# Three ordering edits in a hybrid decoder trunk: the first matmul of each product kept behind the product ahead, the MLP's first weight sum put in front of the operand sums, and the second MLP matrix's first weights issued from GpSimd's queue

## The chip, the cores and the metric

The kernel runs on one core of one Trainium2 chip. The metric is the device time of one execution in microseconds (us), lower is better. Engines are named as the profile names them: PE is TensorE (matmul), ACT is ScalarE, DVE is VectorE, POOL is GpSimd and SP is SyncE. POOL and SP here mostly issue DMA transfers, each into a queue of its own.

## What is computed

One layer: token mixing (a short causal convolution beside forgetting attention, merged by gates), then a squared-ReLU MLP, each with a residual. SEQ is 512, D_MODEL 2048, D_FF 8192, all in float32. The part that matters here, cut down:

```python
merged = gc * conv_branch + ga * attn_branch
x = x + jnp.einsum('bsd,de->bse', merged, w_mix_out[l])          # "mix" below
h = rmsnorm(x, g_mlp[l])
u = jnp.square(jax.nn.relu(jnp.einsum('bsd,df->bsf', h, w_ff1[l])))   # "ff1"
x = x + jnp.einsum('bsf,fd->bsd', u, w_ff2[l])                    # "ff2"
return rmsnorm(x, g_final)
```

## The kernel before

**Seven products for eight.** Each large matrix product is cut in 2x2 quarters and done with seven block products (the Strassen-Winograd form). On the activation side the seven operands are named A11, A12, A22 and the sums S1 to S4; on the weight side the quarters are tiles `x00`, `x01`, `x10`, `x11` (`y..` in ff2), and their sums are made in place by subtractions on DVE (L113). The PSUM accumulators are named `a`, `b`, `c`, `d`, and the results are combined in SBUF tiles `o`.

**Two parts for float32.** Each operand is split in a high part and a low part. `split` (L101) does that: ACT copies the tile to a rounded high part (L103, `th` for weights), and DVE subtracts it from the tile for the low part (L104, `tl`). A product is then three groups of matmuls: high by high and high by the activation's low part, pair by pair, and at the end the weight's low part by the activation's high part. In `mm_rows` these are L172, L173 and L175 (the activation is the stationary operand), in `mm_cols` L153, L155 and L157 (the weight is). So a product needs `th` at its first matmul and `tl` only two thirds on; `th` and `tl` have two buffers each, which come free when the matmuls that read them are done.

**Stages around the change.** The product with `w_mix_out` runs as four column groups of class `Group` (mix groups 0 to 3), the one with `w_ff1` as 16 groups (ff1 groups 0 to 15; the first is `g0`), the one with `w_ff2` as units `unit(seg, cg)`. A mix group runs `head` (A11 into `a`, A12 into `b`) and `tail3` (S1 into `c`, S2 into `a`, S4 into `c`, S3 into `d`, A22 into `a`). S4's low-part result and S2's accumulator meet in `plus` (L116): `o<-c` on ACT (L233), then `o<-a,o` on DVE, and only then A22 may start bank `a` anew. `g0` runs `head`, then `tail2`: S1 into `c`, S3 into `d`, S2 into `a`, S4, A22.

**How ff1 gets its operands.** The result of each mix group is turned (`turn`, transposes on PE into `ptr`), scaled into tiles `f`, and from them class `Mix` makes the operands of ff1: `first_of` is the sum `s1`, `sums` makes the others, `out` splits them. The first three mix groups' shares go through memory (`h_d`, `f_d`) and are loaded again by `begin_part` on POOL's queue; the last group's share is added on chip. For A11 and A12 the loaded rows are split by `split_part` (`A12<-A12 128x1536` on ACT L103 and DVE L104). ff1's weights of `g0` are loaded on POOL's queue too (`g0.queue`, issued at L208). The first weight sum of `g0`, `x00 = x01 - x00`, is in `first_sum`; the mean of the squares, `mean`, is one small matmul (L1308) with a reduction behind it.

**ff1 to ff2.** `put_u` squares the results, makes the sums of ff2's operands in tiles `r`, splits them (`rh` on ACT, `r<-r,rh 128x1792` on DVE L1218) and stores them to `s_d` on POOL's queue. `load_sums` brings them back as `us` tiles (L1337), on POOL's queue as well: part 0 before the last ff1 group's tail, part 1 behind it, then parts 2 and 3. The weights of `unit` come as four tiles of 1 MB each, `y00`, `y10`, `y01`, `y11` (L1438), all on SP's queue before. The first unit runs A11 into `a`, A12 into `b`, S2 into `a` (its weight is `t2 = y11 - (y01 - y00)`), then `d` with `y01 = y11 - y01`.

**What sets the order.** The program is written in a tile framework. A scheduler chooses the order on each engine by its own estimates, within the dependences; `tc.keep_in_program_order(ins)` ties an instruction to the place it has in the code against the others that are tied so, and `tc.issue_after` sets another lower bound. Each engine then runs its list strictly in order, waiting on semaphores. The steps that hang on a product (`after`, class `Steps`) are called when that product's matmuls have been written.

Of the kernel before, what the change touches and what calls it, by code (L numbers as in the profile page):

```python
# [15 lines left out]
P = 128  # L16
# [29 lines left out]
def tile_hybrid_block(ctx: ExitStack, tc, x, g_mix, w_in, b_f, b_gate, conv_w, w_conv_out,  # L46
# [87 lines left out]
        bank(i, "lay")  # L134


    def mm_cols(ps, Sx, hi, lo, first, extra=None):


        ps = ps[0].rearrange("p (j s) -> p j s", j=2)  # L140
        nq = hi.shape[1]
        for part in range(2):
            for q in range(nq):
                Sh, Sl = Sx(q)
                if extra == "first" and part == 0 and q == 0:
                    nc.tensor.matmul(ps[:, 0, :192], hi[:, q, :P], Sh[:, :192], start=True, stop=False,
                                     skip_group_check=True)
                elif extra and extra != "first" and part == 0:
                    extra(q, Sh, hi[:, q, :])
                for j in range(2):  # L150
                    o, js = ps[:, j, :], slice(j * P, (j + 1) * P)
                    if part == 0:
                        nc.tensor.matmul(o, hi[:, q, js], Sh, start=first and q == 0 and j == 0, stop=False,  # L153
                                         skip_group_check=True)
                        nc.tensor.matmul(o, hi[:, q, js], Sl, start=False, stop=False, skip_group_check=True)  # L155
                    else:
                        nc.tensor.matmul(o, lo[:, q, js], Sh, start=False, stop=q == nq - 1, skip_group_check=True)  # L157

    def mm_rows(ps, Sx, hi, lo, first, extra=None, blocks=range(2), qs=None):

        nq, w = hi.shape[1], hi.shape[2]
        for b in blocks:
            o = ps[b][:, :w] if len(ps) == 2 else ps[0][:, b * w:(b + 1) * w]
            begin = first and (b == 0 or len(ps) == 2)
            ts = slice(b * P, (b + 1) * P)
            for part in range(2):
                for q in qs or range(nq):
                    Sh, Sl = (e[:, ts] for e in Sx(q))
                    if extra == "first" and part == 0 and q == 0 and b == 0:
                        nc.tensor.matmul(o[:, :192], Sh, hi[:, q, :192], start=True, stop=False, skip_group_check=True)  # L170
                    if part == 0:
                        nc.tensor.matmul(o, Sh, hi[:, q, :], start=begin and q == 0, stop=False, skip_group_check=True)  # L172
                        nc.tensor.matmul(o, Sl, hi[:, q, :], start=False, stop=False, skip_group_check=True)  # L173
                    else:
                        nc.tensor.matmul(o, Sh, lo[:, q, :], start=False, stop=q == nq - 1, skip_group_check=True)  # L175
# [14 lines left out]
    class Group:  # L190
# [3 lines left out]
        def __init__(self, view, c1, c2, w, ST, mm, banks, put, scale=1.0, extra={}, after=None, shift=SHIFT):  # L194
            self.extra, self.after, self.shift = extra, {} if after is None else after, shift
            self.view, self.cs, self.w, self.ST, self.mm, self.banks = view, (c1, c2), w, ST, mm, banks
            self.put, self.scale, self.at = put, scale, {}
            self.begun, self.queue, self.X = False, nc.sync, {}
# [15 lines left out]
        def run(self, ps, n, src, first):  # L214
            hi, lo = parts([P, self.nq, self.w], self.shift if self.w == HS else 0)
            split(src, hi, lo)
            if n in self.mid:
                self.mm(ps, self.ST(n), hi, lo, first, blocks=(0,))
                self.mid[n]()
                self.mm(ps, self.ST(n), hi, lo, first, blocks=(1,))  # L220
            elif n in self.extra:
                self.mm(ps, self.ST(n), hi, lo, first, self.extra[n])
            else:
                self.mm(ps, self.ST(n), hi, lo, first)
            self.after.get(n, lambda: None)()

        def room(self, i, j):
# [870 lines left out]
    class Mix:  # L1098
# [158 lines left out]
    for g in range(4):  # L1257
# [42 lines left out]
    def factors(common, r):  # L1300
# [122 lines left out]
    def unit(seg, cg, ST):  # L1423
# [9 lines left out]
        for i, j in ((0, 1), (1, 1), (0, 0), (1, 0)) if end else ((0, 0), (1, 0), (0, 1), (1, 1)):  # L1433
# [137 lines left out]
```

## Time and profile before

| | us |
|---|---|
| median of 3 runs (range) | 2443.41 (2442.65 to 2449.26) |
| the profiled execution: its own time | 2446.44 |
| its span in the trace | 2444.7 |
| PE busy | 2408.0 (98%) |
| DVE busy | 2042.6 (84%) |
| ACT busy | 1203.9 (49%) |
| POOL busy | 277.9 (11%) |

The page of the profile gives busy time by engine and the chain that ended last. A row of the timeline reads: start, duration, engine, line, operation, tile written<-tile read, shape, and in brackets how long the engine had been idle before it and what ended that. A matmul's duration is modelled and longer than the distance to the next one; what counts is the distance from start to start, 0.113 us for 256 columns and 0.227 us for 512 where PE waits for nothing. A row of the DMA view ends with the time from issue to landing. A row of the windows view has the stretch, its length, the busy time of PE, of the weight load, DVE, ACT and POOL (each with its count), then the clock that was granted to PE (1.00 is full), the DMA engines' busy share and GB/s. 1.7 us of the execution lie outside the span.

### The profile page before, as it was taken

To read this page: it belongs to the slowest core of one execution; us is meant where nothing else is said; L and a number is where in the kernel's file an instruction comes from. 1 tells how busy PE (TensorE), PEld (TensorE's weight loads), DVE (VectorE), ACT (ScalarE), POOL (GpSimd) and SP (SyncE) were. 2 spreads that over 40 slices of the span, in tenths; PEclk is the share of its full clock that TensorE was granted. 3 is DMA by queue.
4 is the path that set the end of the run, shared out by engine and by line. 5 is a ranking of instruction groups with operands and counts; after the bars stand their busy time and mean duration, and the time that the engine had idled before them with its cause. 6 is when DMAs were issued, how large, how long until landed. Compare 5 with 4: busy or idle time off the path is not lost.

```text
span 2444.7 us, 41518 instructions
## 1 busy us (share of the span) xinstructions
PE 2408.0 (98%) x17800; PEld 2265.2 (93%) x17800; DVE 2042.6 (84%) x1718; ACT 1203.9 (49%) x1233; POOL 277.9 (11%) x446
## 2 busy tenths in 40 slices
PE   8999999999999999999899999999999999999998
PEld 8999899999999999899899999999997888888886
DVE  7987777788888778888889898898888888889898
ACT  6443434345455435355656665666655333333334
POOL 0100000111121111112300000000011001100000
PEclk9999999999999999999999999999999999999999
DMA  7664544445656665657854655646587566655662
GB/s 251 183 191 143 154 134 144 142 154 168 216 170 215 209 208 171 214 163 254 311 198 162 227 204 199 235 171 227 206 301 273 168 240 233 232 194 178 248 224 103
DMA packets 283916, 489.87 MB, mean 200 GB/s; under 512 B 11772, under 2 KB 195188, under 8 KB 283348
## 3 DMA queue, kind: packets, MB, share of 16 engines
q1 hardware_dynamic: 232912, 279.01, 36.0%
q0 software_dynamic: 49952, 207.12, 22.9%
q8 instruction: 139, 2.28, 0.4%
q10 hardware_dynamic: 868, 1.10, 0.1%
q14 instruction: 45, 0.37, 0.0%
HBM read 377.60 MB, written 109.05 MB: 199 GB/s over the span
## 4 chain that ended last, share of the span: by engine, by line
PE 90%; DVE 4%; issue 2%; DMA 2%; ACT 1%; POOL 1%; SPq 0%; DVEq 0%; POOLq 0%; ACTq 0%
PE a L157 6%; PE a L153 6%; PE a L155 6%; PE a L175 5%; PE a L173 5%; PE a L172 5%; PE d L153 5%; PE d L155 5%; PE d L157 5%; PE c L153 4%; PE c L155 4%; PE c L157 4%; PE d L175 3%; PE d L173 3%; PE d L172 3%; PE b L153 3%
## 5 line engine op out<-in xcount | busy, mean ns | idle before, releaser
L103 ACT ACTIVATE th<-x 128x2048 fp32r<-128x2048 f32 (+1 forms) x280 | 537.0, 1918 | 509.2 <-DVE x L113 168.9
L104 DVE TENSOR_TENSOR tl<-x,th 128x2048 fp32r<-128x2048 f32 (+1 forms) x280 | 639.5, 2289 | 168.8 <-ACT th L103 153.8
L113 DVE TENSOR_TENSOR x<-x,x 128x2048 f32<-128x2048 f32 (+1 forms) x160 | 366.1, 2288 | 21.2 <-DMA x<-in_w_in_dram 17.1
L103 ACT ACTIVATE th<-y 128x2048 fp32r<-128x2048 f32 (+1 forms) x109 | 185.4, 1701 | 273.0 <-PE a L173 138.6
L104 DVE TENSOR_TENSOR tl<-y,th 128x2048 fp32r<-128x2048 f32 (+1 forms) x109 | 219.1, 2014 | 30.0 <-ACT th L103 29.6
L172 PE MATMUL a<-th,us 128*128 128x512 f32 x512 | 199.3, 389 | 2.0 <-ACT th L103 2.0
L173 PE MATMUL a<-th,us 128*128 128x512 f32 x512 | 199.2, 389 | 0.0
L153 PE MATMUL c<-S,th 128*128 128x256 f32 x848 | 196.8, 277 | 0.6 <-ACT th L103 0.6
L155 PE MATMUL c<-S,th 128*128 128x256 f32 x848 | 196.4, 277 | 0.0
L153 PE MATMUL a<-S,th 128*128 128x256 f32 x784 | 182.6, 278 | 0.0
L155 PE MATMUL a<-S,th 128*128 128x256 f32 x784 | 181.2, 277 | 0.0
L153 PEld LDWEIGHTS c<-S,th 128*128 128x128 f32 x848 | 159.4, 188 | 1.0 <-ACT th L103 0.7
L155 PEld LDWEIGHTS c<-S,th 128*128 128x128 f32 x848 | 159.4, 188 | 0.0
L155 PEld LDWEIGHTS a<-S,th 128*128 128x128 f32 x784 | 147.4, 188 | 0.0
L153 PEld LDWEIGHTS a<-S,th 128*128 128x128 f32 x784 | 147.3, 188 | 0.0
L175 PE MATMUL a<-tl,us 128*128 128x512 f32 x512 | 137.0, 390 | 0.6 <-DVE tl L104 0.6
L153 PE MATMUL d<-S,th 128*128 128x256 f32 x544 | 128.0, 280 | 0.0
L155 PE MATMUL d<-S,th 128*128 128x256 f32 x544 | 127.3, 279 | 0.0
L155 PE MATMUL b<-A,th 128*128 128x256 f32 x544 | 126.7, 278 | 0.0
L153 PE MATMUL b<-A,th 128*128 128x256 f32 x544 | 126.7, 278 | 0.0
L153 PE MATMUL a<-A,th 128*128 128x256 f32 x544 | 126.3, 278 | 0.0
L155 PE MATMUL a<-A,th 128*128 128x256 f32 x544 | 126.2, 277 | 0.0
(387 smaller groups left out, 6065.8 us busy)
## 6 DMA issues: line engine op xcount, KB each, us to landing
x<-in_w_in_dram SPq DMA_DIRECT2D x86, 1024.0 KB, 6.0
y<-in_w_ff_dram SPq DMA_DIRECT2D x64, 1024.0 KB, 7.0
x<-in_w_ff_dram SPq DMA_DIRECT2D x60, 1024.0 KB, 8.3
us<-s_d POOLq DMA_DIRECT2D x48, 1024.0 KB, 9.9
s_d<-rh POOLq DMA_DIRECT2D x32, 896.0 KB, 5.2
s_d<-r POOLq DMA_DIRECT2D x32, 896.0 KB, 6.1
x<-in_w_mix_out_dram SPq DMA_DIRECT2D x17, 1024.0 KB, 6.7
g_d<-o POOLq DMA_DIRECT2D x32, 256.0 KB, 2.7
```

The source lines that it names most:

```text
L103: a = nc.scalar.activation(out=hi, in_=src, func=AF.Copy, scale=one)
L104: b = nc.vector.tensor_tensor(out=lo, in0=src, in1=hi.bitcast(F32), op=ALU.subtract)
L113: return nc.vector.tensor_tensor(out=out, in0=a, in1=b, op=ALU.subtract)
L153: nc.tensor.matmul(o, hi[:, q, js], Sh, start=first and q == 0 and j == 0, stop=False, skip_group_check=True)
L155: nc.tensor.matmul(o, hi[:, q, js], Sl, start=False, stop=False, skip_group_check=True)
L157: nc.tensor.matmul(o, lo[:, q, js], Sh, start=False, stop=q == nq - 1, skip_group_check=True)
L172: nc.tensor.matmul(o, Sh, hi[:, q, :], start=begin and q == 0, stop=False, skip_group_check=True)
L173: nc.tensor.matmul(o, Sl, hi[:, q, :], start=False, stop=False, skip_group_check=True)
L175: nc.tensor.matmul(o, Sh, lo[:, q, :], start=False, stop=q == nq - 1, skip_group_check=True)
```

## The change

There are three edits.

1. `pinned` keeps the first matmul of a product in program order while `pin[0]` is set. `Group.run` sets it for groups with `in_order`: the four mix groups and `g0`. So a product's first matmul can no longer be put among the matmuls of the product ahead of it.
2. `first_of` of the last mix group is tied behind `first_sum`, so `x00 = x01 - x00` stands ahead of `s1` and what follows it. In mix group 3, `split_part("A12")` moves from the steps after A22 to the steps after S3, ahead of the load of `x10`.
3. The first unit of ff2 issues its four weight loads on POOL's queue; the others stay on SP's.

```diff
+    pin = [False]
+    def pinned(ins):
+        if pin[0]:
+            tc.keep_in_program_order(ins)
+            pin[0] = False
...
-                        nc.tensor.matmul(o, Sh, hi[:, q, :], start=begin and q == 0, stop=False, skip_group_check=True)
+                        pinned(nc.tensor.matmul(o, Sh, hi[:, q, :], start=begin and q == 0, stop=False,
+                                                skip_group_check=True))
...
             split(src, hi, lo)
+            pin[0] = self.in_order
...
+            pin[0] = False
             self.after.get(n, lambda: None)()
...
         def first_of(self):
             self.s1 = pm.tile([P, 2, HS], F32, tag="s1", name="s1")
-            add(self.s1, self.F[1][:, 0], self.F[1][:, 1])
+            return nc.vector.tensor_tensor(out=self.s1, in0=self.F[1][:, 0], in1=self.F[1][:, 1], op=ALU.add)
...
-    g0.queue = nc.gpsimd
+    g0.queue, g0.in_order = nc.gpsimd, True
...
+            after.add("S3", lambda: split_part("A12"))
             after.add("S4", lambda: split_part("A11"))
             after.add("S3", lambda: g0.ahead(1, 0), lambda: begin_part("S3", 3))
             after.add("A22", lambda: g0.ahead(0, 1))
-            after.add("A22", lambda: split_part("A12"))
         group = groups[g]
+        group.in_order = True
...
-    g0.after = Steps(A11=[lambda: g0.ahead(1, 1), turn_waiting, begin_rest, lambda: first_sum_after(mix.added), mix.first_of],
+    g0.after = Steps(A11=[lambda: g0.ahead(1, 1), turn_waiting, begin_rest, lambda: first_sum_after(mix.added),
+                          lambda: tc.keep_in_program_order(mix.first_of())],
...
-            nc.sync.dma_start(out=t, in_=src[i])
+            (nc.gpsimd if seg == cg == 0 else nc.sync).dma_start(out=t, in_=src[i])
```

On each engine the two programs have the same instructions (POOL has SP's four loads besides); only places differ. On PE one row moves before ff2: in the last mix group one `MATMUL c<-th,M` (S4's first) stood between the high-part and the low-part matmuls of S2 (`a<-th,M`, then `a<-tl,M`), and now stands behind all of S2. In ff2's first unit, the four `a<-tl,us` of S2's first row block now stand behind the first four high-part matmuls of its second row block.

**The end of mix group 3.** On ACT the numbers tell tiles apart: `A12_12695` is A12, `o_12840` collects S4's result, `th_12906` (after: `th_12908`) is the high part of `x10`, the weight of A22. Before:

```order
L233 ACTIVATE o_12778<-a_12474 128x512
L1137 ACTIVATE A12_12695<-ptr_12761,cols_97 128x256
L1141 ACTIVATE f_12466<-ptr_12761,cols_97 128x256 x2
L103 ACTIVATE staged_12772<-f_11980 128x512
L233 ACTIVATE o_12840<-c_12640 128x512
L103 ACTIVATE th_12906<-x10_12472 128x2048
L468 ACTIVATE junk_12934,ss2_11038<-o_12840 128x256
```

After:

```order
L244 ACTIVATE o_12778<-a_12474 128x512
L103 ACTIVATE A12_12695<-A12_12695 128x1536
L1148 ACTIVATE A12_12695<-ptr_12761,cols_97 128x256
L1152 ACTIVATE f_12466<-ptr_12761,cols_97 128x256 x2
L103 ACTIVATE staged_12772<-f_11980 128x512
L103 ACTIVATE th_12908<-x10_12472 128x2048
L244 ACTIVATE o_12840<-c_12640 128x512
```

The split of A12's loaded rows came from 16 rows further down to the front of this piece, and `th` of `x10` changed places with `o<-c`. On DVE at the same place, before:

```order
L1138 TENSOR_SCALAR A12_12695<-ptr_12761,cols_97,A12_12695 128x256
L104 TENSOR_TENSOR f_11980<-f_11980,staged_12772 128x512
L116 TENSOR_TENSOR o_12840<-a_12474,o_12840 128x512
L1115 TENSOR_TENSOR o_12840<-o_12840,xr_12633 128x512
L104 TENSOR_TENSOR tl_12907<-x10_12472,th_12906 128x2048
L116 TENSOR_TENSOR o_12703<-d_12845,o_12703 128x512
```

After:

```order
L1149 TENSOR_SCALAR A12_12695<-ptr_12761,cols_97,A12_12695 128x256
L104 TENSOR_TENSOR A12_12695<-A12_12695 128x1536
L104 TENSOR_TENSOR f_11980<-f_11980,staged_12772 128x512
L104 TENSOR_TENSOR tl_12909<-x10_12472,th_12908 128x2048
L116 TENSOR_TENSOR o_12840<-a_12474,o_12840 128x512
L1126 TENSOR_TENSOR o_12840<-o_12840,xr_12633 128x512
```

The read of bank `a` (`o_12840<-a_12474`), which frees it for A22, now stands behind the low part of `x10`.

**The start of ff1, on DVE.** `x00_12833` is the first weight sum of `g0`, `s1_13064` the first operand sum. Before:

```order
L104 TENSOR_TENSOR A12_12695<-A12_12695 128x1536
L1303 TENSOR_REDUCE ms_13127<-ss2_11038 128x4
L116 TENSOR_TENSOR s1_13064<-f_12467 128x512
L104 TENSOR_TENSOR A22_13061<-f_12467,A22_13061 128x512
L113 TENSOR_TENSOR x00_12833<-x01_12984,x00_12833 128x2048
L104 TENSOR_TENSOR S1_12835<-s1_13064,S1_12835 128x512
L113 TENSOR_TENSOR f_12467<-f_12466,f_12467 128x512
L113 TENSOR_TENSOR f_12466<-s1_13064,f_12466 128x512
L1310 TENSOR_REDUCE mean_13134<-mean_13132 128x1
```

After:

```order
L1315 TENSOR_REDUCE ms_13127<-ss2_11038 128x4
L113 TENSOR_TENSOR x00_12833<-x01_12986,x00_12833 128x2048
L1172 TENSOR_TENSOR s1_13064<-f_12467 128x512
L104 TENSOR_TENSOR A22_13061<-f_12467,A22_13061 128x512
L113 TENSOR_TENSOR f_12467<-f_12466,f_12467 128x512
L113 TENSOR_TENSOR f_12466<-s1_13064,f_12466 128x512
L1322 TENSOR_REDUCE mean_13134<-mean_13132 128x1
L104 TENSOR_TENSOR S1_12835<-s1_13064,S1_12835 128x512
```

The weight sum passed `s1` and A22's last rows, and S1's low part fell behind the mean; below this piece the order is the same in both up to `tl_13157<-x00_12833`, the low part of that weight.

**The start of ff2.** On POOL, from the loads of part 0 of `us` on, the order was two `us` loads, a pair of stores (`s_d<-rh`, `s_d<-r`), six `us` loads, another pair of stores. Now it is:

```order
L1350 DMA us<-s_d_79 128x4x512 x2
L1451 DMA y_19876<-in_w_ff_dram 128x4x512
L1451 DMA y_19878<-in_w_ff_dram 128x4x512
L1231 DMA s_d_86<-rh 128x1792
L1232 DMA s_d_86<-r 128x1792
L1350 DMA us<-s_d_79 128x4x512 x2
L1451 DMA y_19880<-in_w_ff_dram 128x4x512
L1451 DMA y_19882<-in_w_ff_dram 128x4x512
L1231 DMA s_d_86<-rh 128x1792
L1350 DMA us<-s_d_79 128x4x512
L1232 DMA s_d_86<-r 128x1792
```

The four `y` loads stand two by two behind the first and the second pair of `us` loads; the last pairs of `us` loads follow with stores among them. On DVE at the same place, before:

```order
L104 TENSOR_TENSOR tl_19917<-y10_19878,th_19916 128x2048
L113 TENSOR_TENSOR r_19775<-r_19775,o_19715 128x256
L113 TENSOR_TENSOR r_19775<-r_19775 128x256
L113 TENSOR_TENSOR t2_19884<-y11_19882,y00_19876 128x2048
L113 TENSOR_TENSOR r_19775<-r_19775 128x256
L113 TENSOR_TENSOR y01_19880<-y11_19882,y01_19880 128x2048
L104 TENSOR_TENSOR tl_19952<-t2_19884,th_19951 128x2048
L1218 TENSOR_TENSOR r_19775<-r_19775,rh_19783 128x1792
L113 TENSOR_TENSOR t2_19884<-y10_19878,t2_19884 128x2048
L104 TENSOR_TENSOR tl_19984<-y01_19880,th_19983 128x2048
```

After:

```order
L104 TENSOR_TENSOR tl_19917<-y10_19878,th_19916 128x2048
L113 TENSOR_TENSOR y00_19876<-y01_19880,y00_19876 128x2048
L1229 TENSOR_TENSOR r_19775<-r_19775,rh_19783 128x1792
L113 TENSOR_TENSOR t2_19884<-y11_19882,y00_19876 128x2048
L113 TENSOR_TENSOR y01_19880<-y11_19882,y01_19880 128x2048
L104 TENSOR_TENSOR tl_19952<-t2_19884,th_19951 128x2048
L104 TENSOR_TENSOR tl_19984<-y01_19880,th_19983 128x2048
```

The sum `y00` was four rows ahead of `tl<-y10` before and now stands behind it, the three short `r` sums ahead of it; the long `r<-r,rh` came ahead of `t2`; and the low part of `y01` follows that of `t2` with nothing between. On ACT two short steps of the last ff1 result (`o<-o,common` and `r<-o 128x512`) came ahead of `th<-y10`.

More of the change, by code (lines that the diff above doesn't have):

```diff
@@ L145, in mm_cols @@
                 if extra == "first" and part == 0 and q == 0:
-                    nc.tensor.matmul(ps[:, 0, :192], hi[:, q, :P], Sh[:, :192], start=True, stop=False,
-                                     skip_group_check=True)
+                    pinned(nc.tensor.matmul(ps[:, 0, :192], hi[:, q, :P], Sh[:, :192], start=True, stop=False,
+                                            skip_group_check=True))
                 elif extra and extra != "first" and part == 0:
@@ L152, in mm_cols @@
                     if part == 0:
-                        nc.tensor.matmul(o, hi[:, q, js], Sh, start=first and q == 0 and j == 0, stop=False,
-                                         skip_group_check=True)
+                        pinned(nc.tensor.matmul(o, hi[:, q, js], Sh, start=first and q == 0 and j == 0, stop=False,
+                                                skip_group_check=True))
                         nc.tensor.matmul(o, hi[:, q, js], Sl, start=False, stop=False, skip_group_check=True)
@@ L171, in mm_rows @@
                     if part == 0:
-                        nc.tensor.matmul(o, Sh, hi[:, q, :], start=begin and q == 0, stop=False, skip_group_check=True)
+                        pinned(nc.tensor.matmul(o, Sh, hi[:, q, :], start=begin and q == 0, stop=False,
+                                                skip_group_check=True))
                         nc.tensor.matmul(o, Sl, hi[:, q, :], start=False, stop=False, skip_group_check=True)
@@ L197, in __init__ @@
             self.put, self.scale, self.at = put, scale, {}
-            self.begun, self.queue, self.X = False, nc.sync, {}
+            self.begun, self.queue, self.X, self.in_order = False, nc.sync, {}, False
             self.pinned, self.mid, self.apart = False, {}, False
```

## The prediction

> **What bounds the kernel now.** I read the page first: busy time by engine and the chain that ended last.
>
> ```profile
> PE 2408.0 (98%) x17800; PEld 2265.2 (93%) x17800; DVE 2042.6 (84%) x1718; ACT 1203.9 (49%) x1233; POOL 277.9 (11%) x446
> PE 90%; DVE 4%; issue 2%; DMA 2%; ACT 1%; POOL 1%; SPq 0%; DVEq 0%; POOLq 0%; ACTq 0%
> ```
>
> PE is the bound, and the change takes no matmul away. So it can only win what PE waits for at the places where it acts. Those I took from the timeline of PE there, by the distance from start to start: 0.113 us for 256 columns, 0.227 for 512.
>
> ```profile
> 1178.16 0.39 PE L172 MATMUL c<-th,M 128*128 128x256 f32 x1 [2.23 <-ACT o L233]
> 1193.37 0.28 PE L172 MATMUL a<-th,M 128*128 128x256 f32 x1
> 1212.29 0.39 PE L153 MATMUL c<-S,th 128*128 128x256 f32 x1 [0.60 <-ACT th L103]
> 1217.61 0.62 PE L157 MATMUL c<-S,tl 128*128 128x256 f32 x3 [1.41 <-DVE tl L104]
> 1221.81 0.53 PE L146 MATMUL d<-S,th 128*128 128x192 f32 x1 [2.05 <-ACT th L103]
> 1834.29 0.50 PE L172 MATMUL a<-th,us 128*128 128x512 f32 x1 [2.04 <-ACT th L103]
> 1837.03 0.50 PE L175 MATMUL a<-tl,us 128*128 128x512 f32 x1 [0.62 <-DVE tl L104]
> 1843.37 0.50 PE L175 MATMUL d<-tl,us 128*128 128x512 f32 x1 [0.60 <-DVE tl L104]
> ```
>
> The bracket is the idle time after the modelled end of the matmul before; the start-to-start distance gives 0.1 to 0.2 us more. Counted that way the seven waits are 2.40 in the mix; 0.73, 1.57 and 2.22 at the start of ff1; 2.21, 0.78 and 0.76 in ff2: 10.7 us, 0.44% of the run. That is the most that the three edits can aim at, and a measurement of this kernel can tell about 0.3% (7.3 us) from no change. The row of 1193.37 has no bracket: A22's product of mix group 3 follows S3's at once.
>
> **Edit 1, the pin.** S4's first matmul (1178.16) stood in front of S2's low-part matmuls and waited for bank `c` to be read by ACT. Behind S2, it leaves those to wait for their own `tl` alone:
>
> ```profile
> 1174.88 2.29 DVE L104 TENSOR_TENSOR tl<-x,th 128x2048 fp32r<-128x2048 f32 x1
> ```
>
> That ends at 1177.17, so they start about 1177.2 instead of 1178.16 plus a step: **-0.96 us**. S4's own start is then no wait any more, since bank `c` is free long before S2's low part is through. PE would reach A22's product at 1193.37 - 0.96 = 1192.4.
>
> **Edit 2, first half: A12's split.** It stood where ACT and DVE had time (first row here) and now stands ahead of the last rows of mix group 3.
>
> ```profile
> 1202.62 1.50 ACT L103 ACTIVATE A<-A 128x1536 fp32r<-128x1536 f32 x1
> 1179.71 0.54 POOL L1092 DMA_DIRECT2D A<-f_d  x1
> A<-f_d POOLq DMA_DIRECT2D x1, 768.0 KB, 8.0
> 1186.08 0.48 ACT L1137 ACTIVATE A<-ptr,cols 128x256 fp32r<-128x256 f32 x1 [1.91 <-DVE A L1138]
> 1187.11 0.84 ACT L1141 ACTIVATE f<-ptr,cols 128x256 f32<-128x256 f32 x2 [0.55 <-DMA h_d<-f]
> 1188.36 0.60 ACT L233 ACTIVATE o<-c 128x512 f32<-128x512 f32 x1
> 1188.84 1.93 ACT L103 ACTIVATE th<-x 128x2048 fp32r<-128x2048 f32 x1
> 1189.11 0.69 DVE L116 TENSOR_TENSOR o<-a,o 128x512 f32<-128x512 f32 x1
> 1190.79 2.29 DVE L104 TENSOR_TENSOR tl<-x,th 128x2048 fp32r<-128x2048 f32 x1 [0.27 <-ACT th L103]
> ```
>
> The rows it splits are issued at 1179.71 and land 8.0 us later, at 1187.7. ACT now waits for them in order, where it had scaled `ptr` at 1186.08. From there: the split 1187.8 to 1189.2 (1.4 to the next start), `A12<-ptr` to 1189.6, `f` and `staged` 1.25 as between 1187.11 and 1188.36, so `th` of `x10` starts at 1190.8 and not at 1188.84, and ends at 1192.7. On DVE the low part of `x10` now stands ahead of `o<-a,o`: 1192.75 to 1195.0, then `o<-a,o` to 1195.65 instead of 1189.8. Until that has read bank `a`, A22's product may not start. Before, that release came 3.6 us ahead of PE and cost nothing; now PE is there at 1192.4 and waits until 1195.7. Against 1193.37 this is **+2.3 us**, and the pin's 0.96 is lost in it. This term is the one on which the sign hangs.
>
> **Edit 2, second half: x00 ahead of the operand sums.** All of ff1's start is 2.3 later. What bounds it now is the load of `x01`, which `x00` needs.
>
> ```profile
> 1194.78 0.68 DVE L1115 TENSOR_TENSOR o<-o,xr 128x512 f32<-128x512 f32 x1
> 1198.10 0.92 POOL L208 DMA_DIRECT2D x<-in_w_ff_dram  x1
> x<-in_w_ff_dram POOLq DMA_DIRECT2D x1, 1024.0 KB, 9.7
> 1211.42 0.28 PE L1308 MATMUL mean<-ms,ones 128*128 128x4 f32 x2
> 1206.73 0.69 DVE L116 TENSOR_TENSOR s<-f 128x512 f32<-128x512 f32 x1 [0.72 <-ACT f L1141]
> 1208.01 2.28 DVE L113 TENSOR_TENSOR x<-x,x 128x2048 f32<-128x2048 f32 x1
> 1210.81 0.68 DVE L113 TENSOR_TENSOR f<-f 128x512 f32<-128x512 f32 x1
> 1212.14 0.15 DVE L1310 TENSOR_REDUCE mean<-mean 128x1 f32<-128x4 f32 x1
> 1215.27 2.28 DVE L104 TENSOR_TENSOR tl<-x,th 128x2048 fp32r<-128x2048 f32 x1
> 1217.47 2.29 DVE L113 TENSOR_TENSOR x<-x,x 128x2048 f32<-128x2048 f32 x1
> ```
>
> It landed at 1207.8, just ahead of `x00` at 1208.01, which ran behind `s1` and A22's rows (1.28 us from 1206.73). On POOL the load stands behind the store (0.7) of the `o` tile that DVE finished at 1195.46 (row of 1194.78), and was issued only at 1198.10. With `o<-a,o` at 1195.0 and three short rows more in between, DVE finishes that tile at 1198.15 now; with the store's 0.7 the load is issued at 1198.85, 0.75 later, and lands at 1208.55. If whatever else held it moves too, it is 2.3 later and the term below grows by 1.1. Then `x00` runs 1208.6 to 1210.85 and its `th` to 1212.9; `b` ends at 1213.6, so the wait of 0.73 at 1212.29 is gone. DVE goes on with `s1` and A22's rows to 1212.1, two `f` sums (1.33, from 1210.81 to 1212.14) to 1213.4, and stands at `mean`, whose matmul comes behind `b`: 1211.42 + 2.3 = 1213.7, with its reduction at about 1214.1. Behind it come S1's low part, `f`, `o<-b`, S3, S2 and S4: from 1212.14 to 1215.27 were 3.13 without S1's 0.6, so `tl` of `x00` starts at 1217.8 and ends at 1220.1. PE, at 1213.85 + 3.7 for 32 matmuls, is there at 1217.5: the wait of 1.57 grows to 2.6, and the low part starts at 1220.1 instead of 1217.61, **+2.5**. `x01` follows on DVE, then its `th` on ACT (1.93), as before: `d<-S` starts at 1224.3 instead of 1221.81. So the head start of `x00` is spent in front of `mean`, and the start of ff1 as a whole is +2.5 (this contains the +2.3); with PE at 98% there is next to no wait behind it that could take it back.
>
> **Edit 3, the y loads.** Before, the last load, `y11`, came late on SP's queue and `t2` waited for it.
>
> ```profile
> y<-in_w_ff_dram SPq DMA_DIRECT2D x1, 1024.0 KB, 17.0
> 1820.39 1.91 ACT L103 ACTIVATE th<-y 128x2048 fp32r<-128x2048 f32 x1
> 1825.93 0.72 ACT L1229 ACTIVATE o<-o,common 128x512 f32<-128x512 f32 x1 [0.21 <-DVE o L116]
> 1826.56 0.62 ACT L1201 ACTIVATE r<-o 128x512 f32<-128x512 f32 x1
> 1829.94 2.29 DVE L113 TENSOR_TENSOR t<-y,y 128x2048 f32<-128x2048 f32 x1 [1.18 <-DMA y<-in_w_ff_dram]
> 1836.89 2.02 DVE L1218 TENSOR_TENSOR r<-r,rh 128x1792 f32<-128x1792 f32 x1
> ```
>
> In POOL's queue `y11` should land some 5 us earlier by its place, but `t2` gains nothing, because of what stands ahead of it: `th` of `y10` (1820.39) is now behind two short ACT steps (0.63 and 0.52 as from 1825.93), so 1821.55 to 1823.45; then on DVE its `tl` 2.2, `y00` 2.2 and the long `r` 1.94: `t2` starts at 1829.8 instead of 1829.94. The wait at 1834.29 stays. The other two go: S2's first low-part matmuls stand 0.9 later on PE, and `tl` of `t2` ends about 1836.5 against a need at 1836.9; `tl` of `y01` follows it at once, ends at 1838.7 and is needed at 1842.6 (before, the long `r` and another `t2`, 1.94 + 2.2, stood between). **-1.5 us.**
>
> **Sum.** +2.5 - 1.5 = +1.0 us on the profiled execution (span 2444.7 and 1.7 around it): 2446.4 to 2447.4. That execution lies 3.0 above the median of the runs shown, so the forecast as a median is 2443.4 + 1.0 = **2444.4**. Own range, with `x01` from 0 to 2.3 late and A12's term from 1 to 3: 2441 to 2448.
>
> **The rivals.**
>
> *The split of A12 does not delay* (chance 0.12). If the rows of `f_d` land a microsecond or two before ACT is there, or DVE still frees bank `a` in time, the mix keeps its -0.96, ff1's start wins 0 to 1, and ff2 -1.5: 2440 to 2441. Against it stands the 8.0 of that load.
>
> *All waits go* (0.06). The change then does what its three edits can at most: -10.7, or about 2433. Against it, each of the seven waits has another cause right behind it in the rows above.
>
> *POOL's queue is too slow: slower* (0.09). At ff2's start the queue carries the `us` loads alone at this rate:
>
> ```profile
> q0 software_dynamic: 397, 1.63, 70.1%
> ```
>
> That is 1.63 MB in the 6 us from 1816, while SP's queue takes the rest. Now 4 MB more must pass in it between the parts of `us`. If it stays at 0.27 MB per us and does not take over what SP's queue leaves, the second pair of loads lands at about 1827, `y01` at 1830.6 and `y11` at 1834.4. It decides as soon as `y11` is later than 1829.8: `t2` is then 4.6 late, and the last `us` parts behind it by as much again: +4 to +8, about 2450.
>
> *The clock* (0.11). The trace shows one stretch at half clock, right behind the wait of 2.22:
>
> ```profile
> 1174.00:1177.40 3.40, 1.93 (x17) 1.73 (x16) 3.17 (x3) 2.59 (x4) 2.34 (x4) 1.00 0.78 281
> 1218.30:1221.70 3.40, 1.46 (x13) 1.25 (x11) 1.46 (x1) 1.85 (x2) 0.00 (x0) 1.00 0.70 287
> 1221.70:1225.10 3.40, 3.29 (x15) 3.29 (x16) 3.31 (x3) 1.30 (x3) 0.00 (x0) 0.50 0.04 14
> ```
>
> A stretch in which PE was busy for 1.46 of 3.40 us was followed by 3.40 at half clock, which costs 1.7; one with 1.93 was not. The forecast's wait of 3.3 ahead of A22 and that of 2.6 ahead of `c`'s low part are as long or longer, so each may cost 1.7 more: +1.7 to +5.1, about 2449 at the worst. The forecast keeps one such stretch, as before; with none it would be 2442.7, inside its own range.
>
> The Trainium skill ("TensorE: Matmul & The Clock Gate", "What's actually happening") says that the clock halves after an idle window of about 3.4 us, with free-running windows. By that rule no wait of 2 to 3.3 us could halve it; this trace disagrees, since it halved after a stretch that was 1.46 us busy. By the rule the sum would be 1.7 less, the old stretch gone, and this rival nil.
>
> **How the numbers follow.** Forecast 0.62, the harmless split 0.12, all waits gone 0.06, POOL's queue 0.09, the clock 0.11. The range 2440 to 2450 takes in the first two, the clock and half of the queue's: 0.88 or so, and narrower would cut into the two slower ones, whose size I know least. Beyond 7.3 us on the fast side lies only the case without waits, 0.06; on the slow side the tail of the queue and of two further half-clock stretches, 0.07; within, 0.87.
>
> **What would show it.** Right: no wait of `c<-th` in S2; ACT's `A<-A 128x1536` starting at its load's landing, near 1187.8; a new wait of about 3 us ahead of A22's first `a<-th`, ended by DVE `o<-a,o`; `c<-S,tl` waiting about 2.6 us; in ff2 one wait of 2 us ahead of S2 and none of 0.7 behind it. Wrong: A22's product without a wait (the sum falls by up to 3 us), `t2` waiting for `y11` (the queue), or a PEclk of 0.50 in more than one stretch of 3.4 us.

## The result, and the profile after

| | before | the change |
|---|---|---|
| median of 11 runs, measured together (us) | 2444.98 | 2450.52 |
| ratio to before, 95% interval | | 1.0020 (1.0011 to 1.0029) |
| span of the profiled execution (us) | 2444.7 | 2450.1 |
| PE busy (us) | 2408.0 | 2409.5 |

The change makes the kernel slower by 0.20%, 4.9 us (2.7 to 7.1), where +1.0 was forecast. That is inside the 0.3% that was given as no change, and its size was missed: on the 2443.4 that the forecast started from it is 2448.3, just above its own range (2441 to 2448) and inside the wide one (2440 to 2450). The page after has the same balance of engines, and the chain has less PE and more waiting in it:

```profile
PE 2409.5 (98%) x17800; PEld 2266.5 (93%) x17800; DVE 2042.8 (83%) x1718; ACT 1203.6 (49%) x1233; POOL 280.8 (11%) x450
...
PE 88%; DVE 4%; issue 3%; DMA 3%; ACT 1%; POOL 1%; DVEq 0%; POOLq 0%; SPq 0%; ACTq 0%
```

The timeline of PE at the same places (from L146 on, lines are 8 to 13 higher than before; `split` and the sums keep theirs):

```profile
1181.10 0.39 PE L184 MATMUL a<-tl,M 128*128 128x256 f32 x1 [2.11 <-DVE tl L104]
...
1198.75 0.38 PE L180 MATMUL a<-th,M 128*128 128x256 f32 x1 [0.77 <-DVE o L116]
...
1217.63 0.38 PE L161 MATMUL c<-S,th 128*128 128x256 f32 x1 [0.69 <-ACT th L103]
...
1224.10 0.38 PE L165 MATMUL c<-S,tl 128*128 128x256 f32 x1 [2.43 <-DVE tl L104]
...
1228.30 0.36 PE L154 MATMUL d<-S,th 128*128 128x192 f32 x1 [2.10 <-ACT th L103]
...
1838.53 0.80 PE L180 MATMUL a<-th,us 128*128 128x512 f32 x1 [3.16 <-ACT th L103]
```

A22's product (1198.75) has the new wait, ended by the read of bank `a`, and `c<-S,tl` the longer one, both at the places forecast. `c<-S,th`, whose wait was to go, still waits. In ff2 the two waits of 0.8 are gone, also as forecast; but the wait ahead of S2 has grown by 1.1 us instead of staying.

**What is chance.** One profile against one profile misleads here. Every program has 17800 matmuls in the same order but for a few, so I compared the distance between the starts of the same matmuls, counted from the first, in all profiles (us):

```
matmuls                  0-100  100-9400 9400-9960 9960-10600 10600-15120 15120-15200
before                   18.96  1136.65    73.10     75.11      513.20      22.29
before again (e5)        18.73  1135.98    74.24     72.53      513.20      20.52
the change               20.91  1137.29    75.75     72.53      513.20      24.49
the change again (e12)   18.39  1140.19    75.97     72.53      513.20      24.31
e1 y on SP               19.04  1138.38    77.52     72.53      513.20      20.67
e2 A12 late              20.15  1136.00    72.60     75.11      513.20      23.09
e3 pins alone            20.55  1137.21    76.66     72.53      513.20      19.55
e4 y alone               20.31  1137.04    72.39     72.53      513.20      23.07
e6 pin and x00           20.67  1136.47    76.44     72.53      513.20      22.45
e7 us part 1 on SP       18.98  1140.01    77.60     73.62      514.72      23.70
e8 A12 alone             20.47  1138.54    74.10     72.53      513.20      20.93
e9 us parts 2, 3 on SP   18.15  1141.76    73.80     72.53      513.20      19.84
e10 y halves             20.22  1137.29    74.80     73.63      513.20      24.55
e11 both                 20.37  1136.50    74.77     72.53      513.20      22.85
```

The third column is the end of mix group 3 and the start of ff1 (1161.6 to 1234.7 in the profile of before), the last one the start of ff2 (1823.0 to 1845.3). The first, second and fourth columns swing by 2.8, 5.8 and 2.6 us with no relation to the edits; they are the execution's. The edits show in the third and the last. One execution of e9 took 4052 us and is left out of its ratio.

### The profile page after: what moved, and what is told of

Its sections match the earlier page's. It is cut to its first block, busy times and chain, and to the rows that moved or that the text cites. A ratio compares the mean times of both kernels' runs of the same rounds, so it can differ in the third digit from the quotient of the medians.

```text
span 2450.1 us, 41512 instructions
## 1 busy us (share of the span) xinstructions
PE 2409.5 (98%) x17800; PEld 2266.5 (93%) x17800; DVE 2042.8 (83%) x1718; ACT 1203.6 (49%) x1233; POOL 280.8 (11%) x450
## 3 DMA queue, kind: packets, MB, share of 16 engines
q8 instruction: 139, 2.28, 0.4%
## 4 chain that ended last, share of the span: by engine, by line
PE 88%; DVE 4%; issue 3%; DMA 3%; ACT 1%; POOL 1%; DVEq 0%; POOLq 0%; SPq 0%; ACTq 0%
PE a L165 6%; PE a L161 6%; PE a L163 6%; PE d L165 5%; PE d L161 5%; PE d L163 5%; PE a L182 5%; PE a L180 5%; PE a L184 5%; PE c L161 4%; PE c L163 4%; PE c L165 4%; PE d L180 3%; PE d L182 3%; PE d L184 3%
```

## The experiments

Two theories of the 5 us stood against each other at the start: A, the loss is local to the starts of ff1 and ff2; B, it comes from the start of the program, which was 2.4 us later in the first profile of the change, or from code placement.

**e1, without edit 3.**

```diff
-            (nc.gpsimd if seg == cg == 0 else nc.sync).dma_start(out=t, in_=src[i])
+            nc.sync.dma_start(out=t, in_=src[i])
```

> The change without edit 3 (the first unit's y loads back on SP's queue). Theory A (the loss is local: about +2.5 us at the start of ff1 and +2 at the start of ff2, where y01 comes late in POOL's queue and the longer wait is followed by half clock): ff2 has its three old waits again (2.2, 0.8, 0.8), no half-clock stretch there, and the time is 2 to 3 us below the change's, 2 to 3 above before. Theory B (the 5 us are not local: they come from the start of the program, 2.4 us later in the profile of the change, or from code placement): the time stays 5 above before whatever ff2's waits are.

Measured: 1.0011 (1.0003 to 1.002), so by these ratios edit 3 carries about half of the loss, within an interval as wide as that half. Its ff2 column is 20.67 against 24.49, and S2's first matmul there waited for 0.58 by the distance of starts:

```profile
1836.33 0.50 PE L180 MATMUL a<-th,us 128*128 128x512 f32 x1 [0.42 <-ACT th L103]
```

That is even less than in the profile of before (2.21): a first sign that the wait of before was one draw among several.

**e2, without A12's move.**

```diff
-            after.add("S3", lambda: split_part("A12"))
...
             after.add("A22", lambda: g0.ahead(0, 1))
+            after.add("A22", lambda: split_part("A12"))
```

> The change with A12's split back behind A22's steps. Theory A: on DVE the read of bank a comes 1.7 us earlier, so the wait of 0.93 us ahead of A22's product goes; the start of ff1 is 0.9 to 1.7 us earlier than in the change, ff2 as in the change (a wait of 3.3 us and half clock behind it). Time 1 to 2 us below the change's. Rival: the low part of x10 ahead of the read of bank a is enough to keep the wait: no difference to the change, under 0.3 us.

Measured: 1.0012 (1.0002 to 1.0021). A22's product follows S3's low part at once:

```profile
1193.22 0.50 PE L184 MATMUL d<-tl,M 128*128 128x256 f32 x3
1193.57 0.28 PE L180 MATMUL a<-th,M 128*128 128x256 f32 x1
...
1835.71 0.50 PE L180 MATMUL a<-th,us 128*128 128x512 f32 x1 [3.04 <-ACT th L103]
```

S2 in ff2 waits as in the change. The rival (the order of the low part alone keeps the wait) falls: on DVE the low part of `x10` stands ahead of the read of bank `a` here too.

**e3, edit 1 alone** (on before, `pinned` with `in_order` set for the mix groups and `g0`).

```diff
+        group.in_order = True
...
-    g0.queue = nc.gpsimd
+    g0.queue, g0.in_order = nc.gpsimd, True
```

> Edit 1 alone on the kernel before. Theory A: the wait inside S2 is shorter (the low part starts up to 0.96 us earlier), A22's product starts without a wait or with one under 0.5, the rest is as before: -1 to 0 us against before, not to be told from no change. Rival: the shorter wait is worth nothing because the read of bank a, now behind the low part of x10, makes A22 wait as long as was won: 0 to +0.5. Theory B: +5 us.

Measured: 1.0008 (0.9999 to 1.0017), which tells little. No wait at A22. The scheduler also put `mean` behind `tl` of `x00` here; `c<-S,tl` did not wait, and `d<-S` waited for 4.40 by the distance of starts instead. What the two waits of 1.57 and 2.22 cost together, this one costs alone and 0.6 more.

**e4, edit 3 alone** (on before; the line of e1 the other way).

> Edit 3 alone on the kernel before. Theory A: y01 lands late, t2 starts 1 us or more later, S2's wait is 3.3 us instead of 2.2, about 3.4 us behind it run at half clock, the two waits of 0.8 are gone: +1 to +2.5 us against before. Rival (the queue costs nothing, the loss of ff2 in the change was chance): -1.5 us, S2's wait 2.2 and no half clock. Theory B: near 0 here and the loss in the start of the program.

Measured: 1.0007 (0.9998 to 1.0017); ff2's column 23.07, that is 0.8 above the profile of before and 2 above the mean of the programs with `y` on SP (below). S2's wait was 3.18, with 3.4 us at half clock behind it, and the two waits of 0.8 were gone. Theory A's mechanism is there, though the time alone does not tell it from no change.

**e5, before again.**

> The kernel before once more, unchanged, for a second profile. Chance only: the time is that of before within the interval. What it tells: how far stages that no edit touches differ from one profile to the next (the start of the program, 2.0 us, and 68 us behind ff1's start in which the distance of matmuls was 4% longer in the profile of before, 2.6 us in all), and where y11 lands on SP's queue against the start of ff2's first product. If the longer distances or the early start come back, they belong to this program; if not, to the execution.

Measured: 0.9997 (0.9988 to 1.0005). Its span is 2440.9, 3.8 us less than in the first profile, with 2.6 of that behind ff1's start and 1.8 in ff2, where `y11` came earlier and S2's first matmul hardly waited:

```profile
1830.58 0.50 PE L172 MATMUL a<-th,us 128*128 128x512 f32 x1 [0.27 <-ACT th L103]
```

So the profile from which I forecast had drawn nearly the worst ff2 of the six profiles with that order (22.29; e6 has 22.45).

**e6, pin and x00** (the change with the edits of e1 and e2 both).

> Edit 1 and the first half of edit 2 (x00 ahead of the operand sums), without A12's move and with the y loads on SP. Theory A (the loss is A12's move, about 3 us, and the y loads, 2 to 4): ff1's start is about 0.5 us earlier than before, ff2 as before; -1 to 0 against before. Rival (each of the edits carries its own loss of 1 to 2): +1.5 to +3.

Measured: 1.0006 (0.9995 to 1.0017): between the two, not settled. `c<-S,tl` waited 2.71; wherever `x00` stands ahead it is 2.3 to 2.7. Its 76.44 in the third column holds 1.24 of a wait among the transposes of a mix result, where no edit acts, and 1.24 of half clock behind S2's wait.

**e7, part 1 of us on SP's queue** (on the change).

```diff
-    load_sums(0, (1,), us0)
+    load_sums(0, (1,), us0, nc.sync)
```

> The whole change, and the second part of us (2 MB) moved from POOL's queue, where it stands ahead of y01 and y11, to SP's. Theory A (y01 is late because it stands behind 2 MB in one first-in first-out queue): y01 lands 4 to 5 us earlier than in the change, y00's sum waits no more for it, S2's wait in ff2 falls from 3.3 to 2 or less with no half clock behind: 1 to 3 us below the change. Rival (all queues share the same engines, which are full there, so what is moved ahead delays the other): y01 earlier but the us part later by as much, S2 waits 2 to 3.3 for us instead of th: within 1 us of the change.

Measured: 1.0023 (1.0014 to 1.0032), no better than the change. My theory failed here: `y01` landed 8.6 us behind the start of `y00`'s low part, 2.3 earlier than in the change, not 4 to 5, and DVE, where `y00`'s sum stands ahead of `tl` of `y10` in this program, waited 5.77 for it:

```profile
1832.88 2.29 DVE L113 TENSOR_TENSOR y<-y,y 128x2048 f32<-128x2048 f32 x1 [5.77 <-DMA y<-in_w_ff_dram]
```

PE then waited 2.36 in `b` for that low part, so the earlier landing bought nothing. This program also has a different order on DVE than the change, so it does not test the queue alone.

**e8, A12's move alone** (on before).

> A12's split ahead on the kernel before, nothing else. Theory A: on DVE 1.75 and the wait for the load's landing stand ahead of the read of bank a: A22's product waits 0 to 1 us, ff1's start is later by up to 1.5, y as before: 0 to +2 against before. Rival: without the pin the read of bank a stands ahead of the low part of x10 and comes in time, so nothing is lost: within 0.3 us in the rows up to ff1's first product.

Measured: 1.0002 (0.9994 to 1.0011). The rival holds: `o<-a,o` stands ahead of the low part of `x10` here, ran at 1195.36, and was done 0.9 before A22 started. **The wait at A22 needs both**: the pin, which turned that pair round, and the split, which delays what is behind it. (Neither alone has it, in e3 and e8; the two together without `x00` were not run.)

**e9, parts 2 and 3 of us on SP's queue behind y11** (on before).

```diff
-            load_sums(0, (2, 3), us0)
+            load_sums(0, (2, 3), us0, nc.sync)
```

> The kernel before, with the last two parts of us put on SP's queue behind y11; the order on PE, ACT and DVE is the same as before. Theory A (at ff2's start the transfers share full DMA engines, and a load is late by what stands ahead of it in its own queue and by what the other queue moves at the time): y11 lands 1 to 3 us earlier against the start of ff2's first product, t2's wait for it shrinks, ff2's first unit loses 0 to 2 us less. Time -2 to 0 against before. Rival (the wait ahead of S2 is set by DVE's own order): y11 earlier, t2 no earlier, no difference in ff2.

Measured: 1.0000 (0.9991 to 1.0009). PE goes from `b` to S2 without a wait:

```profile
1834.07 0.61 PE L175 MATMUL b<-tl,us 128*128 128x512 f32 x2
1834.53 0.39 PE L172 MATMUL a<-th,us 128*128 128x512 f32 x1
```

`t2` started 11.4 behind the start of `y00`'s low part; in the six profiles with all `y` on SP it was 11.1 to 14.0. The mechanism fits, but one profile is inside that spread, and in the time the gain is not to be seen.

**e10, y00 and y10 on POOL's queue, y01 and y11 on SP's** (on before).

```diff
-            nc.sync.dma_start(out=t, in_=src[i])
+            (nc.gpsimd if seg == cg == j == 0 else nc.sync).dma_start(out=t, in_=src[i])
```

> The kernel before with only y00 and y10 on POOL's queue, y01 and y11 alone on SP's; the order on PE, ACT and DVE is that of before. Theory A (in the change y01 is late because it stands in POOL's queue behind two stores and 2 MB of us, not because the loads are on POOL as such): y00 and y10 lands in time, y01 lands no later than before or up to 2 us earlier, no wait over 2.3 us and none of edit 3's loss: -1 to +0.5 against before. Rival (any y load on POOL's queue delays the stores and us behind it by as much): waits for us or for y10 ahead of b or S2, +1 to +2.5.

Measured: 1.0012 (1.0003 to 1.0021): the rival holds in its size, though what came late is `y01`, on SP's own queue. `y01` landed at 1826.7, 8.0 behind the start of `y00`'s low part at 1818.68. SP issued it as early as ever, 8.6 ahead; its transfer took 16.6, against 10.9 to 14.6 with all four on SP's queue. `b` waited 1.86 for `tl` of `y10` and S2 2.48. The transfers in the 6 us from 1816 in this program show how little a load on SP's queue gets while POOL's is full (q0 is POOL's, q1 is SP's; packets, MB, share):

```profile
q0 software_dynamic: 319, 1.85, 74.3%
q1 hardware_dynamic: 315, 0.65, 27.7%
```

Packets are taken from the two in turn, 319 to 315, but POOL's are 5.8 KB and SP's 2.1 KB on average, so SP gets a quarter of the bytes. The Trainium skill ("DMA: Bandwidth & Descriptors", "Queues, rings and completion order") says that a DMA engine goes round the queues that have work, packet by packet; the counts agree, and that the bytes are so unequal is from this trace.

**e11, e9 and e10 together.**

> Both of the two before together: y00 and y10 on POOL's queue, y01 and y11 on SP's with the last parts of us behind them. Theory A: the earliest y11 of all, S2 in ff2 without a wait for it: -2.5 to 0 against before. Rival (DVE's order or the us parts bind): as before.

Measured: 1.0001 (0.9993 to 1.001). Better than e10 in ff2 (22.85 to 24.55), no better than before. With the last `us` parts off POOL's queue `y01` landed 7.7 behind, 0.3 earlier than in e10, and `b` still waits 1.51.

**e12, the change again.**

> The change itself once more for a second profile. Theory A: it is 0.1 to 0.3% above before; the wait ahead of A22's product in mix group 3 is there again (0.9 to 2.8 us), y01 lands about 11 us behind the start of y00's low part on DVE, S2 in ff2 waits 3.2 to 3.4 us. What may differ: which waits are followed by half clock, the start of the program, and the stretch behind ff1's start. Theory B: these waits are not there and the time is still above.

Measured: 1.0022 (1.0013 to 1.0032). The waits are there again:

```profile
1198.31 0.39 PE L180 MATMUL a<-th,M 128*128 128x256 f32 x1 [2.82 <-DVE o L116]
...
1224.27 0.39 PE L165 MATMUL c<-S,tl 128*128 128x256 f32 x1 [2.19 <-DVE tl L104]
...
1838.62 0.80 PE L180 MATMUL a<-th,us 128*128 128x512 f32 x1 [3.06 <-ACT th L103]
```

This program's start was quick (18.39 against 20.91) and the time the same: theory B falls for the start of the program. Code placement was not tried by itself. No kernel tried is faster than before.

## Why the prediction was right and wrong

**The start of ff1: right, +2.9 for +2.5.** The four profiles with edits 1 and 2 whole (the change, e12, e1, e7) have 75.75, 75.97, 77.52 and 77.60 in the third column, mean 76.7; the six whose program is that of before there (before, e5, e4, e9, e10, e11) 72.4 to 74.8, mean 73.9. Single profiles swing as much as this difference: e2 and e6 have the same order on all engines up to ff2, and 72.60 and 76.44, and e3, without A12's move, has 76.66. Much of the swing is half clock, which comes in stretches of 3.4 us (see the rivals): the column holds none of them in e4, three in e3, two in e7, e10 and e11, and one in each of the others. One such stretch costs about 1.4 by an estimate from the change: 18 matmuls were started in it, and 30 fit at full clock. With 1.4 taken off for each, the four lie at 74.3 to 76.1 and the six at 71.7 to 72.8, with e2, e3 and e8 at 71.2 to 72.7. Only e6, at 75.0, is out of line; 1.24 of that is its wait among the transposes, and the rest stays open.

The chain is the one forecast. ACT waited for the landing of A12's rows, and DVE did the low part of `x10` ahead of the read of bank `a`; ACT's rows, then DVE's:

```profile
1190.20 1.49 ACT L103 ACTIVATE A<-A 128x1536 fp32r<-128x1536 f32 x1 [2.00 <-DMA A<-f_d]
...
1193.85 1.92 ACT L103 ACTIVATE th<-x 128x2048 fp32r<-128x2048 f32 x1
```

```profile
1195.80 2.29 DVE L104 TENSOR_TENSOR tl<-x,th 128x2048 fp32r<-128x2048 f32 x1 [0.97 <-ACT th L103]
1198.01 0.68 DVE L116 TENSOR_TENSOR o<-a,o 128x512 f32<-128x512 f32 x1
```

By the distance of starts A22 waited 0.93, 2.98, 2.67 and 2.78 in the four, forecast 3.3; the 0.93 is from the profile in which S2's wait ended late and was followed by half clock, so that PE itself came later. In the ten others it did not wait for bank `a`. The head start of `x00` was spent ahead of `mean`, as forecast: `c<-S,tl` waited 2.59 and 2.35 in the two profiles of the change, forecast 2.6. One step ahead of it was off: the wait of `c<-S,th` (0.73 before) was to go, and was 0.83 and 1.27 in the change and e1, and nothing in e12 and e7.

**The pin: its -0.96 was not there.** S2's wait was 2.28 and 1.46 in the change and 1.79 to 2.26 in e1, e2, e3, e6 and e7, against 1.73 to 2.60 in the seven profiles without the pin: means 2.03 and 2.20. The low-part matmuls did start when their `tl` ended (1181.04 and 1181.10). But the 0.96 was the lead of that end over ACT's read of bank `c` in one profile (1177.17 against 1178.11); in the six other profiles without the pin the lead was 0.0 to 0.6, so there was little to win on average. It cost the sum little, since that gain was to be lost at A22 anyway.

**ff2: wrong, +2.7 for -1.5.** The programs with `y` on SP (before, e5, e1, e3, e6, e8) have 22.29, 20.52, 20.67, 19.55, 22.45 and 20.93 in the last column, mean 21.1; those with edit 3 (the change, e12, e2, e4) 24.49, 24.31, 23.09 and 23.07, mean 23.7. 1.2 of the 2.7 is that the profile I forecast from was a poor draw of its program (22.29 against the mean of 21.1); the rest is +1.5 where -1.5 was forecast.

Profile against profile, the loss has two parts, one on each side of S2's first matmul. From the column's start to that matmul it is 12.38 in the change and 11.27 before: +1.1, the longer wait. From there to the column's end it is 12.11 against 11.02, again +1.1, although the two waits of 0.8 (1.54 together) are gone: 6.8 us at half clock behind the wait took 2.6 there. e12 has 12.29 and 12.01. In e2 and e4 half clock lasted 3.4 us, and the second part is 10.82 and 10.83: what the two waits gave back is nearly all lost to it.

So two steps failed. One is the term of the clock: the forecast kept one stretch at half clock, as before, and ff2 had none of it before. The other is the wait ahead of S2. There the step that failed is the sentence that in POOL's queue `y11` should land some 5 us earlier by its place and that `t2` starts at 1829.8. I looked at the last load and not at the one ahead of it. POOL after, then DVE, from the steps that free the tiles of `y01` and `y11` on, with the low part of `y00` (1819.20) and what follows:

```profile
1806.35 1.49 POOL L1451 DMA_DIRECT2D y<-in_w_ff_dram  x2 [6.81 <-issue]
1810.17 0.56 POOL L1231 DMA_DIRECT2D s_d<-rh  x1 [2.33 <-ACT rh L1228]
1812.85 0.56 POOL L1232 DMA_DIRECT2D s_d<-r  x1 [2.12 <-DVE r L1229]
1813.88 1.52 POOL L1350 DMA_DIRECT2D us<-s_d  x2 [0.48 <-PE d L165]
1815.39 0.75 POOL L1451 DMA_DIRECT2D y<-in_w_ff_dram  x1
1816.35 0.75 POOL L1451 DMA_DIRECT2D y<-in_w_ff_dram  x1 [0.21 <-issue]
```

```profile
1808.32 2.29 DVE L104 TENSOR_TENSOR tl<-x,th 128x2048 fp32r<-128x2048 f32 x1 [0.27 <-ACT th L103]
...
1813.76 2.29 DVE L104 TENSOR_TENSOR tl<-x,th 128x2048 fp32r<-128x2048 f32 x1 [1.21 <-ACT th L103]
1819.20 2.29 DVE L104 TENSOR_TENSOR tl<-y,th 128x2048 fp32r<-128x2048 f32 x1 [3.15 <-ACT th L103]
...
1826.60 2.29 DVE L104 TENSOR_TENSOR tl<-y,th 128x2048 fp32r<-128x2048 f32 x1
1830.10 2.29 DVE L113 TENSOR_TENSOR y<-y,y 128x2048 f32<-128x2048 f32 x1 [1.21 <-DMA y<-in_w_ff_dram]
1832.31 2.02 DVE L1229 TENSOR_TENSOR r<-r,rh 128x1792 f32<-128x1792 f32 x1
1834.24 2.29 DVE L113 TENSOR_TENSOR t<-y,y 128x2048 f32<-128x2048 f32 x1
```

`y01` is the load of 1815.39. POOL issues in order, and it first waits 2.33 and 2.12 for the results that two stores carry, and then for the tile of `us`. So `y01` is issued 3.8 us ahead of the start of `y00`'s low part (1819.20). SP waited for nothing but the tile to come free, when DVE's `tl` ahead had read what was in it, and issued it 8.6 ahead; in the change that `tl` ends at 1810.61, 8.6 ahead as well, and the load stands for 4.8 us behind the others. The waits of SP's loads before, and the landing of `y01` in the change and before:

```profile
SPq L1438 <- DVE tl L104: 34.7, 3, 26.1
...
y<-in_w_ff_dram POOLq DMA_DIRECT2D x1, 1024.0 KB, 14.7
...
y<-in_w_ff_dram SPq DMA_DIRECT2D x1, 1024.0 KB, 14.5
```

The transfer is as long as in the profile of before, but that is a slow draw too: in the six profiles with all `y` on SP it took 10.9 to 14.6, mean 12.7, and in the four with edit 3 14.5 to 14.7. So against the mean the load is 4.8 late by its issue and 1.9 by its transfer. Against the profile of before, issued 4.8 later, it lands 10.9 behind the start of that low part and not 5.9; `y00`'s sum, the long `r` and `t2` follow it without a gap, and `t2` starts 15.0 behind, where it was 13.9 in the profile of before and 12.6 in the mean of the six. In the four profiles with edit 3 that is 14.9 to 15.0 each time. The forecast had DVE's new order as the limit (`y00` 9.6 behind), and that limit would have been right had `y01` come in time. `y11` itself came no earlier either: 13.5 behind in the change, 13.8 in the profile of before and 12.6 in the mean of the six. Its place in a queue could not help it, since its tile comes free when the `tl` of 1813.76 ends, 3.1 ahead of `y00`'s low part; SP issued it then, and POOL 0.3 later.

**The rivals.** The slow queue (+4 to +8) had the right place and a size and a reason that are not the ones measured. From 1818 to 1822 POOL's queue alone moved this (packets, MB, share of the engines):

```profile
q0 software_dynamic: 342, 1.65, 100.9%
```

That is 0.41 MB per us, where both queues together had moved 0.39 before (1.63 and 0.73 MB in 6 us). As a rate the queue is not slow; the load is issued late, and on the way it shares that rate with what else is in the queue.

The clock came about as feared: the sign that was named, a PEclk of 0.50 in more than one stretch of 3.4 us, is there. In the profile of the change three such stretches are at half clock, one behind S2's wait in the mix and two in a row from just ahead of S2's late start in ff2, and the one at `d<-S` is gone:

```profile
1179.12:1182.54 3.42, 1.44 (x12) 1.44 (x13) 3.42 (x3) 3.42 (x6) 2.84 (x6) 1.00 0.91 325
1182.54:1185.95 3.41, 3.41 (x18) 3.41 (x18) 3.41 (x3) 1.31 (x3) 2.37 (x5) 0.50 0.87 196
...
1223.50:1226.91 3.41, 2.10 (x16) 1.91 (x16) 2.75 (x2) 0.57 (x1) 0.00 (x0) 1.00 0.80 328
1226.91:1230.32 3.41, 2.02 (x17) 2.02 (x18) 2.04 (x1) 2.59 (x3) 0.00 (x0) 1.00 0.03 13
...
1834.49:1837.90 3.41, 0.88 (x4) 0.38 (x3) 3.41 (x2) 1.34 (x1) 2.77 (x4) 1.00 1.05 408
1837.90:1841.31 3.41, 2.78 (x7) 2.21 (x8) 3.41 (x3) 2.97 (x3) 0.00 (x0) 0.50 0.93 309
1841.31:1844.73 3.42, 3.42 (x10) 2.65 (x9) 3.42 (x5) 0.46 (x2) 0.00 (x0) 0.50 1.01 343
```

The stretches are cut like this because, in each profile, all changes of the granted clock lie on one grid of 3.413 us, whose phase differs from execution to execution. On that grid there is a pattern. In the fourteen profiles, from 40 to 2430 us, 25 grid stretches at full clock had PE busy for 1.54 us or less, and half clock followed each of them; 13 had 1.55 to 1.70, and it followed 4 of them; it followed none of the others. (Busy time goes by modelled ends, so the bounds belong to this view.) So a wait of some 2 us brings half clock when it falls inside one grid stretch, and none when the grid divides it: the wait of 2.27 at `d<-S` was parted at 1226.91, and both stretches still had over 2 us busy. So the waits that half clock follows change from one profile of a program to the next: in e12 they were A22's and ff2's. The Trainium skill ("TensorE: Matmul & The Clock Gate", "What's actually happening") has the window run freely, which fits this grid; that it must be idle for about 3.4 us does not fit any of these stretches.

**The sum.** +2.9 and +2.7 are 5.6; measured were 4.9 (2.7 to 7.1) and 5.4 (3.2 to 7.8). By undoing one edit at a time, the time falls by 2.2 us (edit 3, e1) and 2.0 (A12's move, e2), each of them 0.9 or 0.8 thousandths with an interval as wide, so that neither is clear of noise by the times alone; what shows them are the waits and the two columns. What the pin and `x00` cost or bring by themselves (e3, e6) stays open within about 2 us.

## What to carry to other kernels

A load that is moved to another engine's queue is issued when that engine gets to it: before counting bandwidth, list what stands ahead of it in that engine's order and what each of those waits for. An edit that ties one order and an edit that moves work can be harmless alone and cost a wait together, so look at the pairs that the scheduler turned round. A wait of PE can cost more than its length, since half clock may follow it; whether it does depends on where it falls on a grid that no edit controls, so a forecast should carry that as a chance for each wait. And where the effects are of a few us, take a second profile of the kernel before: the spread of the term in question may be larger than the term.

## What the hardware showed beside this

In two of the fourteen profiles (before and e2) matmuls came 4% slower for some 65 us behind ff1's start, at a granted clock of 1.00, 342 against 355 in 40 us; the first row is of before, the second of the change:

```profile
1260.00:1300.00 40.00, 40.00 (x342) 40.00 (x341) 33.68 (x26) 24.31 (x25) 2.12 (x4) 1.00 0.55 195
```

```profile
1266.00:1306.00 40.00, 40.00 (x355) 40.00 (x354) 35.28 (x27) 25.75 (x27) 2.12 (x4) 1.00 0.56 198
```

What sets it off was not found. Two other profiles (e7, e10) have about 1.1 us of it there, and e7 another 1.5 later.
